# Queries, keys and probabilities of the mixers turned through HBM instead of on TensorE

## The chip, the core and the metric

One core of a Trainium2 chip runs the whole program. The metric is the device time of one execution in microseconds. The kernel before takes 2475.66 us (median of 3 runs, 2475.55 to 2479.15).

## The reference, cut to what matters

Two layers work on 256 tokens of width 2048. Each layer has a mixer, a cross-attention into 256 memory tokens and a feed-forward network (FFN), each added to `x`.

```python
# layer 0: proj = rms_norm(x) @ w_in_ab -> rq, rk, rv, rg (retention), nq, nk, nv (neighbourhood attention)
ret = rms_norm(fwd + bwd, ret_g) * silu(rg)              # 8 heads of 128, chunkwise retention both ways
na  = softmax(norm(nq) @ norm(nk).T * scale + bias) @ nv # 8 heads of 128
x = x + concat(ret, na) @ w_out_ab
# layer 1: proj = rms_norm(x) @ w_in_c -> q, k, v (8 heads, two queries and two keys of 128, values of 256)
a = softmax(q0 @ k0.T * scale + alibi) - lam * softmax(q1 @ k1.T * scale + alibi)
x = x + (rms_norm(a @ v, out_g) * (1 - lam_init)) @ w_out_c
# both layers: cross-attention (4 heads), then (silu(h @ w_g) * (h @ w_u)) @ w_ffn_out
```

A product on TensorE sums over the partitions, so the left operand must lie with its summed axis there. Projections come out with tokens on the partitions. Queries, keys, probabilities and head outputs therefore have to be turned before their next product.

## The kernel before, in words

**The products.** `gemm` (line 297) goes through 864 units. A unit is 256 rows of the weights by 512 columns, for both token tiles `t`: 12 matrix products of 128x128 by 128x512 (lines 321 to 323), since every operand is a high part and a low remainder (`hi`, `lo`; `wh`, `wl`) and three of the four partial products are summed. `prepare` (line 269) loads 1 MB of weights for two units (`raw`), casts a unit's high part on ScalarE (line 292, `wh`) and subtracts for the low part on VectorE (line 293, `wl`). It stands `LOOK` = 2 units ahead in the program. `wh` and `wl` have three buffers each, so the cast of unit k can start once TensorE is through with unit k-3, which is two units before unit k begins.

**The side work.** Everything between the products is a generator in `Side` (line 33). After each unit `pump` (line 63) lets one ready task make one step; a `yield n` puts the next step off by n units. At most `CAP` = 5 tasks are under way. `drain` finishes tasks at once where a later product needs them. The engines run their queues in order, so an instruction that waits holds all that stands behind it on its engine. The order in each queue is made when the program is built.

**The turn on TensorE.** `turn` (line 340) issues four 128x128 transposes into a PSUM tile `pt`. `heads_T` (line 459) does that twice for each group of queries or keys, `transpose_p` (line 541) once for a head's probabilities, `diff_head` (line 699) once more for a head's output in layer 1, `gate_T` (line 607) twice for a group of gated outputs. ScalarE and VectorE then make the high and low part out of `pt`.

**The move through HBM.** `regroup` (line 377) turns without TensorE, and before it serves the inputs of cross-attention and of the FFN's two projections (`feed`, `act_T`): VectorE transposes 32x32 squares (line 389, `zz`), SyncE writes them to HBM (line 391, `zd`), `LAND` = 2 units later GpSimd's queue reads them back by four DMAs, one for each 32 partitions (line 394), and `MOVE` = 5 units after the start ScalarE and VectorE make high and low part from `zz`.

**GpSimd's other duty.** `rsqrt_mean` (line 334) has the power -1/2 of each norm done on GpSimd, and VectorE's next instruction (line 487) waits for it.

Of the kernel before, what the change touches and what calls it, by code (L numbers as in the profile page):

```python
# [26 lines left out]
LAND, MOVE = 2, 5  # L27
# [5 lines left out]
class Side:  # L33
# [3 lines left out]
    CAP = 5  # L37
# [44 lines left out]
def trunk_kernel(  # L82
# [129 lines left out]
    def pair(which, name):  # L212
        hi = big.tile([P, 16, T], F32R, tag=f"{which}h", name=f"{name}h")
        lo = big.tile([P, 16, T], F32R, tag=f"{which}l", name=f"{name}l")
        return hi, lo
# [81 lines left out]
    def gemm(kts, src, epi, gate=None, steps=1, wide=False):  # L297
        hi, lo = src
        w2, rows, cols, order = plan[at["phase"]]
        at["phase"] += 1  # L300
        nu = 2 * len(rows)
        accs, left = {}, {}
        for b, u in order:
            side.drain((gate or {}).get(u, ()))
            if b not in accs:
                pools = ((ps_acc, f"acc{t}") for t in range(2))
                if wide and b in (2, 3):
                    pools = ((ps_t, "pt"), (ps_t, "pt")) if b == 2 else ((ps_a, "pa"), (ps_a, "pa"))
                accs[b] = [q.tile([P, NB], F32, tag=tag, name=f"acc{t}") for t, (q, tag) in enumerate(pools)]
                left[b] = nu  # L310
            while len(ahead) <= LOOK and at["unit"] < len(units):
                prepare()
            wh, wl = ahead.popleft()
            acc = accs[b]
            first, left[b] = left[b] == nu, left[b] - 1
            last = left[b] == 0
            for t in range(2):
                ts = slice(t * P, (t + 1) * P)
                for j in range(2):
                    kt = kts[u // 2] + 2 * (u % 2) + j  # L320
                    nc.tensor.matmul(acc[t], lhsT=hi[:, kt, ts], rhs=wh[:, j], start=first and j == 0, stop=False)  # L321
                    nc.tensor.matmul(acc[t], lhsT=hi[:, kt, ts], rhs=wl[:, j], start=False, stop=False)  # L322
                    nc.tensor.matmul(acc[t], lhsT=lo[:, kt, ts], rhs=wh[:, j], start=False, stop=last and j == 1)  # L323
            if last:
                epi(b, acc)
            side.pump(steps)
# [21 lines left out]
    def gained(dst, kt, src, g):  # L348
        hi, lo = dst[0][:, kt], dst[1][:, kt]
# [27 lines left out]
    def regroup(srcs, room=""):  # L377


        if room == "m8":  # L380
            both = m8.tile([P, 2, 4 * T], F32, tag="m8", name="zz")
            zt, zT = both[:, 0], both[:, 1]
        elif room:
            zt, zT = (qk.tile([P, 4 * T], F32, tag=room + x, name="zz") for x in "hl")
        else:
            zt, zT = (vp.tile([P, 4 * T], F32, tag="v" + x, name="zz") for x in "hl")
        zt = zt.rearrange("p (j k t b) -> p j k t b", j=4, k=4, t=2)
        for t in range(2):
            nc.vector.transpose(zt[:, :, :, t], srcs[t].rearrange("p (k j a) -> p j k a", j=4, a=32))
        zd = dram.tile([4, 32, 4, T], F32, name="zd")  # L390
        nc.sync.dma_start(zd.rearrange("i a j n -> (i a) (j n)"), zt.rearrange("p j k t b -> p (j k t b)"))
# [5 lines left out]
        return zT.rearrange("p (i k t b) -> p i k t b", i=4, k=4, t=2)  # L397
# [11 lines left out]
    def feed(dst, b, srcs, gi, layer, ssr, room):  # L409
# [5 lines left out]
        for k in range(4):  # L415
            g = gain(gi, layer, 4 * b + k)
            hi, lo = (x[:, 4 * b + k].rearrange("p (t i b) -> p t i b", t=2, i=4) for x in dst)
# [6 lines left out]
    def feed_x(dst, b, gi, layer, ssr, room=""):  # L424

        return [side.add(feed(dst, b, x_block(b), gi, layer, ssr, room))] * 2
# [32 lines left out]
    def heads_T(zs, dst, g):  # L459
# [21 lines left out]
    def normed_T(acc, rstd, gc, name, wait=4):  # L481
# [12 lines left out]
        return d, side.add(heads_T(zs, d, head_gain(gc)), wait)  # L494

    def plain_T(acc, rstd, name, mul):
        zs = evac(acc, rstd)
        d = turned(name)
        return d, side.add(heads_T(zs, d, mul), 3)
# [48 lines left out]
    def attend(g, h, dst, kt, bias=None):  # L548
# [10 lines left out]
        yield g.get("wait", 4)  # L559
        pT = transpose_p(pr)  # L560
# [5 lines left out]
        split(dst[0][:, kt], dst[1][:, kt], po)  # L566
# [40 lines left out]
    def gate_T(zs, oT, kt, g):  # L607
        for u in range(2):
            pt = turn(zs, u)
            gained_pair(part(oT, slice(kt + 2 * u, kt + 2 * u + 2)), pt, g)  # L610
            yield 0

    def retention_na(j, hT, rstd, oT, gate):
        groups = [{"n": 0} for gi in range(4)]
        groups[0]["tb"] = side.add(na_bias(j, 0, groups[0], hT[0][:, 4, 0:16].bitcast(F32)), 6)
        tails = []

        def epi(b, acc):
            if b < 12:
                gi, part = b // 3, b % 3  # L620
                g = groups[gi]
                if gi < 2:
                    if part == 0:
                        g["q"], g["tq"] = normed_T(acc, rstd, c_naq + j, "qT")
                    elif part == 1:
                        g["k"], g["tk"] = normed_T(acc, rstd, c_nak + j, "kT")
                        side.drain([g["tb"], small[0]])
                        heads = [side.add(attend(g, h, oT, 8 + gi * 4 + h, bias=g["bias"]), cond=prepared(g))
# [5 lines left out]
                elif part == 0:  # L634
                    side.drain(small)
                    g["q"], g["tq"] = plain_T(acc, rstd, "qT", 1.0)
                elif part == 1:
                    g["k"], g["tk"] = plain_T(acc, rstd, "kT", SCALE)
# [6 lines left out]
            else:  # L645
# [9 lines left out]
                tails.append(side.add(gate_T(zs, oT, gi * 4, head_gain(c_ret + j)), 2))  # L655
# [6 lines left out]
    def diff_head(g, hh, h, j, oT):  # L662
# [17 lines left out]
        yield 3  # L680
        aT = transpose_p(p0)
# [14 lines left out]
        for t in range(2):  # L696
            nc.vector.tensor_scalar(do[:, t], po[:, t], rr[:, t:t + 1], None, op0=ALU.mult)
# [8 lines left out]
    def diff_attention(j, hT, rstd, oT, gate):  # L706
        groups = [{} for _ in range(4)]

        def epi(i, acc):
            b, part = i // 3, i % 3  # L710
            g = groups[b]
            if part == 0:
                g["q"], g["tq"] = normed_T(acc, rstd, c_dq + j, "qT")
            elif part == 1:
                g["k"], g["tk"] = normed_T(acc, rstd, c_dk + j, "kT")
                g["tasks"] = [side.add(diff_head(g, hh, 2 * b + hh, j, oT), cond=prepared(g)) for hh in range(2)]
# [42 lines left out]
    for layer in range(2):  # L759
# [37 lines left out]
        tasks = [t for b in range(4) for t in feed_x(hT, b, 1, layer, ssr, ("", "", "qT", "m8")[b])]  # L797
# [15 lines left out]
        xo = (xo[:, 0], xo[:, 1])  # L813
# [6 lines left out]
        def epi_xo(b, acc):  # L820
# [3 lines left out]
            else:  # L824
                tasks.extend(feed_x(hT, b, 3, layer, ssr, ("", "", "qT", "kT")[b]))
# [4 lines left out]
        def act_T(aT, zs, kt):  # L830
            zT = yield from regroup(zs)
            for t in range(2):
                split(*(x[:, kt:kt + 4, t * P:(t + 1) * P].rearrange("p k (i b) -> p k i b", i=4) for x in aT),
                      zT[:, :, :, t].rearrange("p i k b -> p k i b"))
# [76 lines left out]
```

## Time and profile before

| what | value |
|---|---|
| time, median of 3 | 2475.66 us |
| profiled execution: time / span | 2475.84 us / 2474.1 us |
| TensorE busy | 2456.3 us (99%) |
| VectorE / ScalarE / GpSimd busy | 60% / 48% / 6% |
| DMA | 511.82 MB, mean 207 GB/s |
| granted TensorE clock | 1.000 |

The span runs from the first to the last instruction; 1.7 us lie around it. Busy is the time in which an engine has an instruction in work. TensorE's products overlap: one is recorded with some 390 ns although the next one starts 227 ns after it, so what a product costs is read from the distance of starts, not from its recorded length.

### The profile page before, as it was taken

How to read it: one execution, taken by the hardware profiler on the slowest of the kernel's cores; microseconds unless marked ns; L12 is line 12 of the kernel's file. 1: busy time of each engine (PE TensorE's matmuls, PEld its weight loads, DVE VectorE, ACT ScalarE, POOL GpSimd, SP SyncE). 2: the span in 40 equal slices, each digit the busy share in tenths (PEclk: the TensorE clock that was granted, in tenths of full speed). 3: DMA queues.
4: the chain of work that ended last, by engine and by line, in shares of the span. 5: the costliest groups of instructions: out<-in, count | busy, mean ns of one | idle time of the engine just before them, and what ended most of it. 6: DMA issues, size and time to landing. Idle time of an engine off the chain costs nothing.

```text
span 2474.1 us, 28641 instructions
## 1 busy us (share of the span) xinstructions
PE 2456.3 (99%) x11184; PEld 2037.1 (82%) x11184; DVE 1475.7 (60%) x1833; ACT 1187.0 (48%) x1538; POOL 138.2 (6%) x215
## 2 busy tenths in 40 slices
PE   8999999999999999999999999999999999999999
PEld 6888888888888888888888888888888888888887
DVE  6775565675655555555567766767655545555554
ACT  6554464564443444444455555655544444443443
POOL 1000001010000000000010000010100000000000
PEclk9999999999999999999999999999999999999999
DMA  8555567656765666566674555675766656665665
GB/s 288 177 169 179 175 226 245 214 192 213 233 216 200 205 212 225 194 198 226 225 241 164 170 170 168 212 249 171 237 222 210 215 188 214 228 206 200 207 217 175
DMA packets 250184, 511.82 MB, mean 207 GB/s; under 512 B 11328, under 2 KB 11968, under 8 KB 250048
## 3 DMA queue, kind: packets, MB, share of 16 engines
q1 hardware_dynamic: 239568, 484.47, 58.5%
q0 software_dynamic: 8320, 23.08, 4.1%
q10 hardware_dynamic: 2160, 2.44, 0.3%
q8 instruction: 87, 1.43, 0.2%
q14 instruction: 49, 0.40, 0.0%
HBM read 486.88 MB, written 23.07 MB: 206 GB/s over the span
## 4 chain that ended last, share of the span: by engine, by line
PE 92%; DMA 3%; DVE 3%; ACT 1%; POOL 1%; issue 0%; ACTq 0%; SPq 0%; POOLq 0%; DVEq 0%
PE acc L322 30%; PE acc L321 30%; PE acc L323 30%; DMA zz<-zd 2%; DVE wl L293 1%; DMA zd<-zz 1%; PE pt L345 1%; ACT wh L292 0%; PE pt L545 0%; PE pa_s L437 0%; PE pa_s L436 0%; DVE x_sb L741 0%; PE pa_s L435 0%; POOL zz L394 0%; PE pa_r L595 0%
## 5 line engine op out<-in xcount | busy, mean ns | idle before, releaser
L293 DVE TENSOR_TENSOR wl<-raw,wh 128x1024 fp32r<-128x1024 f32 (+1 forms) x865 | 1053.7, 1221 | 870.8 <-ACT wh L292 870.4
L292 ACT CAST wh<-raw 128x1024 fp32r<-128x1024 f32 (+1 forms) x865 | 909.1, 1051 | 1158.2 <-PE acc L323 1132.8
L322 PE MATMUL acc<-wl,hTfh 128*128 128x512 f32 x1408 | 547.9, 389 | 0.6 <-DVE wl L293 0.6
L323 PE MATMUL acc<-wh,hTfl 128*128 128x512 f32 x1408 | 547.7, 389 | 0.0
L321 PE MATMUL acc<-wh,hTfh 128*128 128x512 f32 x1408 | 547.7, 389 | 0.0
L321 PE MATMUL acc<-wh,hTh 128*128 128x512 f32 x832 | 332.0, 399 | 9.8 <-ACT wh L292 8.3
L322 PE MATMUL acc<-wl,hTh 128*128 128x512 f32 x832 | 325.7, 391 | 0.9 <-DVE wl L293 0.9
L323 PE MATMUL acc<-wh,hTl 128*128 128x512 f32 x832 | 325.8, 392 | 0.0
L322 PEld LDWEIGHTS acc<-wl,hTfh 128*128 128x128 f32 x1408 | 264.3, 188 | 56.2 <-DVE wl L293 1.4
L323 PEld LDWEIGHTS acc<-wh,hTfl 128*128 128x128 f32 x1408 | 264.3, 188 | 54.9
L321 PEld LDWEIGHTS acc<-wh,hTfh 128*128 128x128 f32 x1408 | 264.3, 188 | 54.9
L322 PE MATMUL acc<-wl,aTh 128*128 128x512 f32 x704 | 274.0, 389 | 0.2 <-DVE wl L293 0.2
L323 PE MATMUL acc<-wh,aTl 128*128 128x512 f32 x704 | 273.9, 389 | 0.0
L321 PE MATMUL acc<-wh,aTh 128*128 128x512 f32 x704 | 273.9, 389 | 0.0
L321 PEld LDWEIGHTS acc<-wh,hTh 128*128 128x128 f32 x832 | 157.2, 189 | 40.0 <-ACT wh L292 8.3
L323 PEld LDWEIGHTS acc<-wh,hTl 128*128 128x128 f32 x832 | 156.7, 188 | 34.0
L322 PEld LDWEIGHTS acc<-wl,hTh 128*128 128x128 f32 x832 | 157.2, 189 | 31.2 <-DVE wl L293 1.8
L394 POOL DMA_DIRECT2D zz<-zd x160 | 87.3, 552 | 1589.9 <-DMA zd<-zz 1410.9
L322 PEld LDWEIGHTS acc<-wl,aTh 128*128 128x128 f32 x704 | 132.1, 188 | 28.2 <-DVE wl L293 0.8
L321 PEld LDWEIGHTS acc<-wh,aTh 128*128 128x128 f32 x704 | 132.1, 188 | 27.5
L323 PEld LDWEIGHTS acc<-wh,aTl 128*128 128x128 f32 x704 | 132.1, 188 | 27.3
L321 PE MATMUL acc<-wh,oTh 128*128 128x512 f32 x256 | 100.2, 392 | 0.0
(189 smaller groups left out, 1940.3 us busy)
## 6 DMA issues: line engine op xcount, KB each, us to landing
raw<-in_w_ffn_in SPq DMA_DIRECT2D x176, 1024.0 KB, 5.1
raw<-in_w_ffn_out SPq DMA_DIRECT2D x88, 1024.0 KB, 5.1
raw<-in_w_in_ab SPq DMA_DIRECT2D x55, 1024.0 KB, 5.2
raw<-in_w_in_c SPq DMA_DIRECT2D x48, 1024.0 KB, 5.2
zd<-zz SPq DMA_DIRECT2D x40, 512.0 KB, 3.8
zz<-zd POOLq DMA_DIRECT2D x160, 128.0 KB, 5.4
raw<-in_w_out_ab SPq DMA_DIRECT2D x16, 1024.0 KB, 5.1
raw<-in_w_xkv SPq DMA_DIRECT2D x16, 1024.0 KB, 5.0
```

The costliest lines, as they stand in the source:

```text
L292: nc.scalar.copy(wh[:, js], raw[:, rs])
L293: nc.vector.tensor_sub(wl[:, js], raw[:, rs], wh[:, js])
L321: nc.tensor.matmul(acc[t], lhsT=hi[:, kt, ts], rhs=wh[:, j], start=first and j == 0, stop=False)
L322: nc.tensor.matmul(acc[t], lhsT=hi[:, kt, ts], rhs=wl[:, j], start=False, stop=False)
L323: nc.tensor.matmul(acc[t], lhsT=lo[:, kt, ts], rhs=wh[:, j], start=False, stop=last and j == 1)
L345: nc.tensor.transpose(pt[:, j, t * P:(t + 1) * P], srcs[t][:, c:c + P], ident)
L394: nc.gpsimd.dma_start(zT[32 * j:32 * j + 32].rearrange("a (i n) -> a i n", i=4), zd[:, :, j].rearrange("i a n -> a i n"))
```

## The change

`heads_T`, `attend`, `diff_head` and `gate_T` take a `room`. With a room they turn by `regroup` with `wait=SLOW` (8 units from start to the split; `gate_T`'s too); without one they turn on TensorE as before. Queries and keys of all four groups of layer 0 and of groups 0 to 2 of layer 1 go through HBM, as do the probabilities of the eight neighbourhood heads, the probabilities and outputs of heads 0 to 5 of layer 1, and the first group of gated outputs. Group 3 of layer 1 and the second gate group stay on TensorE. Squares of two 128-wide tiles (`nk=2`) are half as large as those before. `CAP` is 7. Operands (`pair`) become four tiles of four 128-row blocks; blocks of `oT` that aren't filled yet are the rooms. Two scalings in `diff_head` move from VectorE to ScalarE.

```diff
-LAND, MOVE = 2, 5
+LAND, MOVE, SLOW = 2, 5, 8
-    CAP = 5
+    CAP = 7
+    class Pair:
+        def blk(self, b):
+            if b not in self.blocks:
+                self.blocks[b] = tuple(big.tile([P, 4, T], F32R, tag=f"{self.which}{x}{b}", name=f"{self.name}{x}")
+                                       for x in "hl")
+            return self.blocks[b]
+    def regroup(srcs, room="v", nk=4, wait=MOVE):
+        zt, zT = room_for(room, nk * T)
+        zv = zt.rearrange("p (j k t b) -> p j k t b", j=4, k=nk, t=2)
+        for t in range(2):
+            nc.vector.transpose(zv[:, :, :, t], srcs[t].rearrange("p (k j a) -> p j k a", j=4, a=32))
+        zd = dram.tile([4, 32, 4, nk * 64], F32, tag=f"zd{nk}", name="zd")
+        nc.sync.dma_start(zd.rearrange("i a j n -> (i a) (j n)"), zt)
         yield LAND
         for j in range(4):
             nc.gpsimd.dma_start(zT[32 * j:32 * j + 32].rearrange("a (i n) -> a i n", i=4),
                                 zd[:, :, j].rearrange("i a n -> a i n"))
-        yield MOVE - LAND
+        yield wait - LAND
+    def split_moved(dst, zT):
+        for t in range(2):
+            split(*(x[:, :, t * P:(t + 1) * P].rearrange("p k (i b) -> p k i b", i=4) for x in dst),
+                  zT[:, :, :, t].rearrange("p i k b -> p k i b"))
-    def heads_T(zs, dst, g):
+    def heads_T(zs, dst, g, room=None):
+        if room:
+            zT = yield from regroup(zs, room, wait=SLOW)
+            if g is not None:
+                flat = zT.rearrange("p i k t b -> p (i k t b)")
+                nc.scalar.activation(flat, flat, AF.Copy, scale=g)
+            split_moved(dst, zT)
+            return
...
-        yield g.get("wait", 4)
-        pT = transpose_p(pr)
+        if room:
+            zT = yield from regroup([pr[:, t] for t in range(2)], room, 2, SLOW)
+            pT = tuple(pp.tile([P, 2, T], F32R, name="p" + x) for x in "hl")
+            split_moved(pT, zT)
+        else:
+            yield g.get("wait", 4)
+            pT = transpose_p(pr)
...
+        spare = [oT.which + x for x in "01"]
-                        g["q"], g["tq"] = normed_T(acc, rstd, c_naq + j, "qT")
+                        g["q"], g["tq"] = normed_T(acc, rstd, c_naq + j, "qT", spare[0])
...
+        def spare(b, x):
+            return oT.which + x if b < 3 else None
-                g["q"], g["tq"] = normed_T(acc, rstd, c_dq + j, "qT")
+                g["q"], g["tq"] = normed_T(acc, rstd, c_dq + j, "qT", spare(b, "3"))
...
-            nc.vector.tensor_scalar(p1[:, t], p1[:, t], r1[:, t:t + 1], None, op0=ALU.mult)
+            nc.scalar.activation(p1[:, t], p1[:, t], AF.Copy, scale=r1[:, t:t + 1])
...
+        if room:
+            zT = yield from regroup([do[:, t] for t in range(2)], room, 2, SLOW)
+            for e in range(2):
+                ze = zT[:, :, e].rearrange("p i t b -> p i (t b)")
+                nc.scalar.activation(ze, ze, AF.Copy, scale=head_gain(c_do + 2 * j + e))
+            split_moved(oT.at(2 * h, 2), zT)
+            return
```

On TensorE, where the queries of layer 0's first group are turned (z the normed queries, pt the PSUM tile), the kernel before has this between the end of a unit and the next unit:

```order
L322 MATMUL acc_554<-wl,hTh 128x512
L323 MATMUL acc_554<-wh,hTl 128x512
L345 MATMUL pt<-ident,z 128x128 x4
L321 MATMUL acc_553<-wh,hTh 128x512
L322 MATMUL acc_553<-wl,hTh 128x512
```

At the same place the changed kernel has:

```order
L335 MATMUL acc_564<-wl,hTh 128x512
L336 MATMUL acc_564<-wh,hTl 128x512
L334 MATMUL acc_563<-wh,hTh 128x512
L335 MATMUL acc_563<-wl,hTh 128x512
L336 MATMUL acc_563<-wh,hTl 128x512
```

The four transposes are gone from between the units; 50 such fours are gone from the whole queue (64 stand alone between two units before, 14 after), and the first scores of that group stand after 26 units instead of 21.

On ScalarE, in the same group, from the keys to the first head's probabilities (kTh the keys' high part, pr the probabilities, ph their high part, vh the values), before:

```order
L445 ACTIVATE kTh<-pt,gcol 128x512
L292 CAST wh<-raw 128x1024
L537 ACTIVATE pr,se<-pr,mx 128x256 x2
L292 CAST wh<-raw 128x1024
L537 ACTIVATE pr,se<-pr,mx 128x256 x2
L292 CAST wh<-raw 128x1024
L509 ACTIVATE vh<-acc_553,ssxr 128x512
```

In the changed kernel:

```order
L488 ACTIVATE zz<-zz,gcol 128x1024
L540 ACTIVATE vh<-acc_564,ssxr 128x512
L306 CAST wh<-raw 128x1024
L453 CAST kTh<-zz 128x4x128 x2
L306 CAST wh<-raw 128x1024 x2
L568 ACTIVATE pr,se<-pr,mx 128x256 x2
L306 CAST wh<-raw 128x1024
L568 ACTIVATE pr,se<-pr,mx 128x256 x2
L306 CAST wh<-raw 128x1024 x3
L453 CAST ph<-zz 128x2x128 x2
```

The reads of `zz`, which wait for a DMA, now stand among the casts of the weights. All 35 moves of the mixers stand so; from the VectorE transposes to ScalarE's first read there are 5 to 7 casts of the weights for a full square and 3 to 6 for a half one.

On GpSimd, at the start of layer 1 (rr the norm's power, rrd that of a head's output, zz<-zd the reads from HBM), before:

```order
L394 DMA zz<-zd 32x4x256 x4
L334 TENSOR_TENSOR rr<-rr,mhalf 128x8 x2
L334 TENSOR_TENSOR rrd<-rrd,mhalf 128x2 x2
L334 TENSOR_TENSOR rr<-rr,mhalf 128x8 x2
L334 TENSOR_TENSOR rrd<-rrd,mhalf 128x2 x2
```

In the changed kernel:

```order
L412 DMA zz<-zd 32x4x256 x4
L347 TENSOR_TENSOR rr<-rr,mhalf 128x8
L412 DMA zz<-zd 32x4x256
L347 TENSOR_TENSOR rr<-rr,mhalf 128x8
L412 DMA zz<-zd 32x4x256 x7
L412 DMA zz<-zd 32x4x128 x4
L347 TENSOR_TENSOR rr<-rr,mhalf 128x8
L412 DMA zz<-zd 32x4x128 x4
L347 TENSOR_TENSOR rrd<-rrd,mhalf 128x2
L412 DMA zz<-zd 32x4x256 x4
```

Reads that wait for `zd` now stand ahead of the powers in one queue, where before the powers had it to themselves.

## Rows read from the trace of the kernel before

**Rows 1.** The page: busy time of each engine, and the granted clock.

```profile
PE 2456.3 (99%) x11184; PEld 2037.1 (82%) x11184; DVE 1475.7 (60%) x1833; ACT 1187.0 (48%) x1538; POOL 138.2 (6%) x215
...
PEclk9999999999999999999999999999999999999999
```

**Rows 2.** Waits of TensorE: waited for, us in total, times, longest us.

```profile
PE acc L321 <- ACT wh L292: 8.3, 1, 8.3
PE acc L322 <- DVE wl L293: 2.2, 6, 0.5
PE pa_o L436 <- DVE pl L430: 1.6, 1, 1.6
PE acc L321 <- DVE z L475: 1.5, 2, 0.8
```

**Rows 3.** Groups by line and shape, TensorE, the transposes: xcount | busy us, mean ns | idle.

```profile
L345 PE MATMUL pt<-ident,z 128*128 128x128 f32 x160 | 23.6, 272 | 0.0
...
L545 PE MATMUL pt<-ident,pr 128*128 128x128 f32 x96 | 14.7, 272 | 0.0
...
L702 PE MATMUL pt<-ident,do 128*128 128x128 f32 x32 | 4.8, 272 | 0.0
...
L345 PE MATMUL pt<-ident,sg 128*128 128x128 f32 x16 | 2.4, 272 | 0.0
```

**Rows 4.** Timeline of TensorE in the FFN, first and thirteenth product: start us, us.

```profile
640.05 0.39 PE L321 MATMUL acc<-wh,hTfh 128*128 128x512 f32 x1
...
642.77 0.39 PE L321 MATMUL acc<-wh,hTfh 128*128 128x512 f32 x1
```

**Rows 5.** Timeline of TensorE in layer 0's mixer, a unit and its turn.

```profile
65.64 0.48 PE L321 MATMUL acc<-wh,hTh 128*128 128x512 f32 x1
65.96 0.39 PE L322 MATMUL acc<-wl,hTh 128*128 128x512 f32 x1
...
68.50 0.60 PE L345 MATMUL pt<-ident,z 128*128 128x128 f32 x4
68.85 0.48 PE L321 MATMUL acc<-wh,hTh 128*128 128x512 f32 x1
```

**Rows 6.** Timelines of VectorE, SyncE, GpSimd, ScalarE: one square of the FFN.

```profile
675.76 1.29 DVE L389 STREAM_TRANSPOSE zz<-sg 128x512 f32<-128x512 f32 x2
...
677.08 0.34 SPq L391 DMA_DIRECT2D zd<-zz  x1
...
681.36 2.17 POOL L394 DMA_DIRECT2D zz<-zd  x4 [40.04 <-DMA zd<-zz]
...
688.53 1.05 ACT L292 CAST wh<-raw 128x1024 fp32r<-128x1024 f32 x1 [1.67 <-PE acc L323]
689.48 1.14 ACT L429 CAST aTh<-zz 128x512 fp32r<-128x512 f32 x2
...
690.76 1.29 DVE L430 TENSOR_TENSOR aTl<-zz,aTh 128x512 fp32r<-128x512 f32 x2
```

**Rows 7.** The chain of waits where three squares follow each other: start us, us.

```profile
541.06 6.83 DMA zd<-zz
...
548.46 1.62 POOL zz L394 x3
550.08 9.15 DMA zz<-zd
...
559.34 0.52 ACT hTfh L419
559.88 2.20 DVE hTfl L421 x8
...
563.30 0.50 PE acc L322
```

**Rows 8.** Lines 394 and 391, all DMAs: length and time to landing, min/median/max.

```profile
L394 POOL DMA_DIRECT2D zz<-zd x160: 550/550/595, 402.9 to 2413.1; - x160
DMA to landing us min/median/max: 2.8/5.4/9.4
...
L391 SPq DMA_DIRECT2D zd<-zz x40: 338/338/339, 399.6 to 2406.9; - x40
DMA to landing us min/median/max: 2.6/3.8/7.3
```

**Rows 9.** Stretches (layer 0's mixer, then layer 1's): us, PE, PEld, DVE, ACT, POOL, clock, DMA, GB/s.

```profile
8.00:357.00 349.00, 346.00 (x1656) 288.23 (x1657) 225.26 (x323) 184.11 (x269) 18.75 (x17) 1.00 0.63 204
...
1263.00:1560.00 297.00, 295.71 (x1433) 246.91 (x1433) 205.72 (x313) 157.57 (x247) 21.07 (x19) 1.00 0.53 175
```

**Rows 10.** Timeline of VectorE and TensorE at the end of the first keys' norm.

```profile
62.29 1.29 DVE L475 TENSOR_TENSOR z<-acc,rr 128x512 f32<-128x512 f32 x2
...
56.03 0.47 PE L321 MATMUL acc<-wh,hTh 128*128 128x512 f32 x1 [0.72 <-DVE z L475]
```

**Rows 11.** Tile rr on GpSimd, and who waited for it (us, times).

```profile
L334 POOL TENSOR_TENSOR rr<-rr,mhalf x18: 1630/1636/2723, 53.3 to 1700.8; 128x8 f32<-128x8 f32 x18
...
  DVE rr L487: 27.8, 16
```

More of the change, by code (lines that the diff above doesn't have):

```diff
@@ L209, in lambdas, with __init__, at @@
         yield
[L212 to L215, printed above, removed]
+    class Pair:
+        def __init__(self, which, name):
+            self.which, self.name, self.blocks = which, name, {}
+        def blk(self, b):
[3 more added lines that the diff above has]
+            return self.blocks[b]
+        def at(self, kt, n=None):
+            k = kt % 4
+            return tuple(x[:, k if n is None else slice(k, k + n)] for x in self.blk(kt // 4))
+    pair = Pair
     side = Side()
@@ L319, in gemm @@
                 for j in range(2):
[L320 to L323, printed above, removed]
+                    hi, lo = src.at(kts[u // 2] + 2 * (u % 2) + j)
+                    nc.tensor.matmul(acc[t], lhsT=hi[:, ts], rhs=wh[:, j], start=first and j == 0, stop=False)
+                    nc.tensor.matmul(acc[t], lhsT=hi[:, ts], rhs=wl[:, j], start=False, stop=False)
+                    nc.tensor.matmul(acc[t], lhsT=lo[:, ts], rhs=wh[:, j], start=False, stop=last and j == 1)
             if last:
@@ L493, in normed_T, with plain_T @@
         d = turned(name)
-        return d, side.add(heads_T(zs, d, head_gain(gc)), wait)
-    def plain_T(acc, rstd, name, mul):
+        return d, side.add(heads_T(zs, d, head_gain(gc), room), 0 if room else 4)
+    def plain_T(acc, rstd, name, mul, room):
         zs = evac(acc, rstd)
         d = turned(name)
-        return d, side.add(heads_T(zs, d, mul), 3)
+        return d, side.add(heads_T(zs, d, mul, room))
     def prepared(g):
@@ L605, in ret_head, with gate_T @@
                 head_scale(ro[t], ro[t], rr, t)
[L607 to L611, printed above, removed]
+    def gate_T(zs, oT, kt, g, room):
+        yield from heads_T(zs, oT.at(kt, 4), g, room)
     def retention_na(j, hT, rstd, oT, gate):
+        spare = [oT.which + x for x in "01"]
         groups = [{"n": 0} for gi in range(4)]
-        groups[0]["tb"] = side.add(na_bias(j, 0, groups[0], hT[0][:, 4, 0:16].bitcast(F32)), 6)
+        groups[0]["tb"] = side.add(na_bias(j, 0, groups[0], hT.blk(1)[0][:, 0, 0:16].bitcast(F32)), 6)
         tails = []
@@ L654, in epi @@
                     zs.append(sg)
-                tails.append(side.add(gate_T(zs, oT, gi * 4, head_gain(c_ret + j)), 2))
+                tails.append(side.add(gate_T(zs, oT, gi * 4, head_gain(c_ret + j), ("qT", None)[gi]), 2 * gi))
         gemm(KT4, hT, epi, gate=gate)
@@ L712, in epi @@
             if part == 0:
-                g["q"], g["tq"] = normed_T(acc, rstd, c_dq + j, "qT")
+                g["q"], g["tq"] = normed_T(acc, rstd, c_dq + j, "qT", spare(b, "3"))
             elif part == 1:
-                g["k"], g["tk"] = normed_T(acc, rstd, c_dk + j, "kT")
-                g["tasks"] = [side.add(diff_head(g, hh, 2 * b + hh, j, oT), cond=prepared(g)) for hh in range(2)]
+                g["k"], g["tk"] = normed_T(acc, rstd, c_dk + j, "kT", spare(b, "2" if b < 2 else "3"))
+                g["tasks"] = [side.add(diff_head(g, hh, 2 * b + hh, j, oT, oT.which + str(b + 1) if b < 3 else None), cond=prepared(g)) for hh in range(2)]
             else:
@@ L796, in trunk_kernel @@
         ssr = new_ss("ssx")
-        tasks = [t for b in range(4) for t in feed_x(hT, b, 1, layer, ssr, ("", "", "qT", "m8")[b])]
+        tasks = [t for b in range(4) for t in feed_x(hT, b, 1, layer, ssr, ("v", "v", "qT", "m8")[b])]
         g = {"wait": 3}
```

63 lines of the change are left out of this document (32 added, 31 removed).

## The prediction

> **What bounds the kernel now.** I read the page first: TensorE is busy for 2456.3 of 2474.1 us at a granted clock of 1.0 (the 2.4 GHz level) in every slice, VectorE 60%, ScalarE 48% [rows 1]. So the next view is who makes TensorE wait: four rows, of which the first (8.3 us) is the start of the program; the others add up to 5.3 us [rows 2]. The kernel is bounded by what stands in TensorE's queue. A busy TensorE can hide what an instruction costs, since products overlap, so the timeline comes third, and there the reader should look at distances of starts. In the FFN the thirteenth product starts 642.77 - 640.05 = 2.72 us after the first [rows 4]: a unit without side work. In layer 0's mixer a unit that ends in a turn takes 68.85 - 65.64 = 3.21 us [rows 5]. A turn of four transposes therefore costs 3.21 - 2.72 = 0.49 us of TensorE. The four take 0.35 us until the next product starts (68.85 - 68.50), and the rest goes to that product, whose successor comes 0.32 us after it instead of 0.23 [rows 5]. The group rows would mislead: 272 ns for one transpose [rows 3] is its recorded length, not its cost.
>
> **What is removed.** By the order 50 fours leave the stretches between units: 28 of queries and keys (14 groups of two), 14 of probabilities, 6 of head outputs, 2 of gated outputs; 200 of the 304 transposes in [rows 3]. On the path that sets the end that is 50 x 0.49 = 24.5 us. Nothing else in TensorE's queue changes in number, and the products that stay keep their shapes. The profiled execution took 2475.84 us, 0.2 us over the median of the three runs, so without any new wait the time would be 2475.84 - 24.5 = 2451.3 us.
>
> A page speaks of the same operation: the Trainium skill's "TensorE: Matmul & The Clock Gate", section "Part 4: PE-mode transpose", gives some 275 ns for a 128x128 transpose inside a kernel. The recorded length agrees [rows 3], but the distance of starts does not [rows 5]; by the page 200 x 0.275 = 55 us would go, an estimate that gives 2421 us.
>
> **What is added on the other engines.** 35 moves: 15 full squares (as large as those of before) and 20 half ones. VectorE gets 1.29 us of transposes and 1.29 us of subtractions for a full square [rows 6] and about half for a half one; even with nothing set off for what it no longer reads from PSUM that is 15 x 2.58 + 20 x 1.29 = 65 us. In the two mixers VectorE is busy for 225.3 + 205.7 = 431 of 646 us and ScalarE for 342 [rows 9]; 65 more makes 77%, and ScalarE's share (casts of 1.14 us for a full square, scalings, the two moved from VectorE) stays under 65%. That work is hidden by the products. The bytes are hidden too: 15 x 1 MB + 20 x 0.5 MB on a DMA share of 0.63 and 0.53 [rows 9]. What can cost is waiting, in three queues.
>
> **The first keys of each layer.** Their scores are the one place where TensorE takes up a square almost as soon as it lands. In layer 0 the keys' norm ends at 62.29 + 1.29 = 63.6 us, and unit 16 starts at 56.03 [rows 10]. The transposes of queries and keys put 2 x 1.29 us in front: 66.2. A quiet square needs 689.48 - 677.05 = 12.4 us from the end of its transposes to ScalarE's read [rows 6]; one among close neighbours needed 559.34 - 541.06 = 18.3 [rows 7]. Then come scaling (1.05, as the cast of the same shape), casts (1.14) and the last subtraction (0.65): ready between 81.4 and 87.3. TensorE reaches the scores 10 units after unit 16, at 83.2. It waits for 0 to 4.1 us; with two squares 6 us apart I take the middle, 1.8. Layer 1 opens in the same pattern (units 456 to 466): together 3.6 us.
>
> **The half squares.** Behind ScalarE's read of a square stand the casts of the weights, and behind those the products. ScalarE's cast is two units ahead, so a read may stand for 5.44 - 1.05 = 4.4 us before TensorE notices. In the FFN the read stands six casts behind the transposes and comes 12.4 us after them, 3.9 us under six units. By that measure a read three casts behind comes after 4.3 us, four casts behind after 7.0, five after 9.7. In the order 5 half squares stand at three, 10 at four, 5 at five or six. No row shows a half square: its bounds are the shortest landings with GpSimd's four issues, 2.6 + 0.6 + 2.17 + 2.8 = 8.2 us [rows 6, 8], and the 18.3 of [rows 7]. I take 10.5, since the nearest row is the quiet full square (12.4), with the same number of issues and half the bytes. At four casts 10.5 - 7.0 = 3.5 lies inside the reserve. At three 10.5 - 4.3 - 4.4 = 1.8 is left; but the mixers' units are longer (297 / 96 = 3.1 us [rows 9]), which gives back up to 1.1 over three. I take 1.0 each: 5 us. The full squares of later groups stand at 5 to 7 and have units to spare before their scores: nothing.
>
> **GpSimd's queue.** Reads that wait for `zd` now stand ahead of the norms' powers. VectorE already waits 27.8 / 16 = 1.7 us for each power [rows 11] and its lead is 5.44 - 1.05 - 1.23 = 3.2 us, so a short hold is hidden; I take nothing, with 0 and the rival below as ends. SyncE's `zd` stands between the loads of `raw`, six casts ahead of use as the FFN's do now, where TensorE shows no wait for a load [rows 2].
>
> Sum: 2475.84 - 24.5 + 3.6 + 5 = 2459.9, say **2460 us**, its own range 2452 to 2468.
>
> **The rivals.**
> (a) *Late half squares on ScalarE; slower.* If a half square takes 14 us (between the quiet row and [rows 7]), those at three casts lose 14 - 8.7 = 5.3 each and those at four 14 - 11.4 = 2.6 each: 26 + 26, with 5 for the first keys 57, which gives 2508 us. It decides from about 12 us on: 5 x 3.3 + 10 x 0.6 + 3.6 = 26 eats the gain. For it: [rows 7], and that in layer 1 two heads and the next group's queries and keys move within some 25 us. Against: there three full squares lay 5 us apart, and the mixers have the lightest DMA share [rows 9]. 10 in 100.
> (b) *Powers held behind reads.* Eight norms have their power directly behind reads in GpSimd's queue. Each hold is up to the median landing of `zd`, 3.8 [rows 8]: 3.8 + 1.7 - 3.2 = 2.3 us for TensorE, 18 in all, hence 2478 us, no change. For it: the queue is in order. Against: the reads are issued two units after `zd`, which is longer than 3.8. 11 in 100.
> (c) *The moves are as short as their best.* With 8.2 us for any square no read outlasts the reserve and the first keys are in time: 2451 us. Against: medians of 3.8 and 5.4 [rows 8]. 15 in 100. The Trainium skill has this in "DMA: Bandwidth & Descriptors", section "Anatomy of one DMA — SWDGE (gpsimd) path": 2.0 us plus bytes at 436 GB/s, by which 64 KB would land in 2.15 us and the sum would again be 2451, an estimate. The trace does not agree: 128 KB took 5.4 us in the median and 2.8 at the least.
> (d) *The transposes cost their recorded length.* 200 x 0.272 = 54 us less, 2421. Against it is every distance of starts in [rows 5]. 2 in 100.
> (e) *Later side work piles up.* The scores come some 5 units later than before, and what is unfinished at the end of a projection is drained without products in between. The order shows no such heap; the last head of layer 1 is turned at unit 547 instead of 543, its reader is at 549. Were a whole drain exposed there, with one full square's 12.4 us, it would be 2472 us. 2 in 100.
>
> **How the numbers follow.** The forecast has 60 in 100. What a measurement of this kernel can tell from no change is about 0.2%, 5 us: below 2470.7 is faster, above 2480.6 slower. Faster: 60 + 15 + 2 + a rest of 1 from (b) = 78. Same: 10 of (b) and (e) = 12. Slower: (a), 10. The range from 2450 to 2476 leaves out (a), (d) and most of (b) and is wide because the half square has no row.
>
> **What would show it.** TensorE's groups: 104 transposes are left, and a plain unit is still 2.72 us. Waits of TensorE: first scores of each layer 0 to 4 us, casts of the weights (wh, wl) together about 5. The reads and writes of half squares land in the time between them that I took (10.5 us from transposes to landing); over 12 the forecast falls to (a). Powers on GpSimd: VectorE's wait for rr stays near 1.7 each; at 4 or more (b) holds. If the units around the moves grow above 2.72 us without a named wait, the forecast is wrong in a way that none of these has.

## The result and the profile after

The changed kernel takes 2487.31 us (median of 4 runs, 2482.08 to 2490.55), the kernel before on the same chip 2475.61. The ratio is 1.0041, 95% interval 1.0029 to 1.0052: slower, where 2460 us and faster was forecast. The profiled execution took 2482.08 us, 6.2 more than that of before. One execution of e1 below (5048.88 us) and one of e2 (4118.33 us, at a mean clock of 0.556) lie far off and are left out of the ratios; e2's only trace is of that one, so nothing is read from it.

TensorE's own work shrank as planned. First the page's row of busy times and its clock (PE is TensorE, PEld its weight loads, DVE VectorE, ACT ScalarE, POOL GpSimd), then the groups of transposes that are left (columns as in [rows 3]):

```profile
PE 2443.0 (98%) x10984; PEld 2018.3 (81%) x10984; DVE 1493.0 (60%) x1885; ACT 1211.9 (49%) x1609; POOL 223.0 (9%) x355
...
PEclk9999999999999999999999999999999999999999
```

```profile
L358 PE MATMUL pt<-ident,z 128*128 128x128 f32 x48 | 7.1, 273 | 0.1
L576 PE MATMUL pt<-ident,pr 128*128 128x128 f32 x40 | 6.3, 272 | 0.0
...
L358 PE MATMUL pt<-ident,sg 128*128 128x128 f32 x8 | 1.4, 279 | 0.2 <-DVE sg L687 0.2
L748 PE MATMUL pt<-ident,do 128*128 128x128 f32 x8 | 1.2, 272 | 0.0
```

Of the 304 transposes of [rows 3] 104 are left, 200 are gone, and PE has 200 instructions fewer than in [rows 1]. The time came back, most of it as waits: TensorE's span less its busy time is 2480.3 - 2443.0 = 37.3 us, and was 2474.1 - 2456.3 = 17.8. Here are TensorE's waits, then ScalarE's (waited for: us in total, times, longest us):

```profile
PE acc L334 <- ACT wh L306: 17.7, 7, 8.4
PE acc L335 <- DVE wl L307: 11.0, 21, 0.8
PE pa_s L460 <- DVE kTl L454: 1.7, 2, 1.0
```

```profile
ACT zz L741 <- DMA zz<-zd: 28.4, 6, 6.7
...
ACT zz L488 <- DMA zz<-zd: 21.5, 9, 7.7
...
ACT ph L453 <- DMA zz<-zd: 17.0, 7, 5.1
ACT do L736 <- POOL rrd L347: 10.6, 8, 3.0
```

In [rows 2] TensorE waited once for `wh` (8.3 us, the start of the program) and 2.2 us for `wl`. Now it waits 9.4 us more for `wh` and 8.8 more for `wl`. And ScalarE, which casts `wh`, stands 66.9 us at squares that have not landed: 28.4 at head outputs (line 741), 21.5 at queries and keys (488), 17.0 at probabilities (453). The fourth line (736) came with the scalings that moved to ScalarE; it is no part of the loss, for e1 below keeps it (9.4 us) and loses nothing.

The worst place shows how the one becomes the other. It is the keys of layer 0's second group. First the chain of waits (start us, us), then the timelines of ScalarE and TensorE (start us, us, engine, line, operation, in brackets the idle time before and what ended it), then TensorE's part in stretches of 5 us (us, PE, PEld, DVE, ACT, POOL, granted clock, DMA share, GB/s):

```profile
141.07 6.77 DMA zd<-zz
...
148.41 1.35 POOL zz L412 x3
150.09 10.02 DMA zz<-zd
```

```profile
151.46 1.05 ACT L306 CAST wh<-raw 128x1024 fp32r<-128x1024 f32 x1 [1.67 <-PE acc L336]
160.22 1.15 ACT L488 ACTIVATE zz<-zz,gcol 128x1024 f32<-128x1024 f32 x1 [7.71 <-DMA zz<-zd]
161.28 1.25 ACT L540 ACTIVATE vh<-acc,ssxr 128x512 fp32r<-128x512 f32 x2
162.42 1.04 ACT L306 CAST wh<-raw 128x1024 fp32r<-128x1024 f32 x1
```

```profile
163.51 0.80 PE L334 MATMUL acc<-wh,hTh 128*128 128x512 f32 x1 [3.93 <-ACT wh L306]
...
165.79 0.63 PE L334 MATMUL acc<-wh,hTh 128*128 128x512 f32 x1
166.22 0.63 PE L335 MATMUL acc<-wl,hTh 128*128 128x512 f32 x1
```

```profile
155.00:160.00 5.00, 4.58 (x21) 3.46 (x19) 0.00 (x0) 0.00 (x0) 0.00 (x0) 1.00 0.97 253
160.00:165.00 5.00, 1.03 (x2) 0.52 (x3) 2.92 (x4) 4.78 (x7) 0.00 (x0) 0.84 0.06 22
165.00:170.00 5.00, 5.00 (x12) 3.90 (x13) 3.19 (x4) 1.52 (x3) 0.00 (x0) 0.50 0.33 86
```

The square landed 19.1 us after its transposes (141.04 to 160.1), beside weight loads at a DMA share near 1. ScalarE reached its read 6 casts behind the transposes by its queue (two of them ran before VectorE was through) and stood 7.71 us. On release the scaling and two casts of the values came first; the cast of the weights that would have been due at 151.46 + 2.72 = 154.2 started at 162.42, 8.2 us late. TensorE noticed 3.93 of them. Then a second price fell due: the granted clock went to 0.84 and 0.50 (the 1.2 GHz level), and products followed each other at 0.43 us (165.79 to 166.22) instead of 0.23 (2.72 / 12 by [rows 4]). By their starts two units and the one after them took 7.8 us more than such units take otherwise (6.81 and 6.12 instead of 2.72, and 3.74, where the next one with the same six products of scores takes 3.46). 4.4 of that was waiting (3.93 and 0.46), the other 3.4 the clock. Nowhere else in this execution was the granted clock under 1.00.

VectorE's wait for the norms' powers did not grow (28.0 us in 16 times here, 27.8 in [rows 11]).

### The profile page after: what moved, and what is told of

Same layout as the page of the kernel before. It is cut to its first block, busy times and chain, and to the rows that moved or that the text cites. A ratio compares the mean times of both kernels' runs of the same rounds, so it can differ in the third digit from the quotient of the medians.

```text
span 2480.3 us, 28762 instructions
## 1 busy us (share of the span) xinstructions
PE 2443.0 (98%) x10984; PEld 2018.3 (81%) x10984; DVE 1493.0 (60%) x1885; ACT 1211.9 (49%) x1609; POOL 223.0 (9%) x355
## 4 chain that ended last, share of the span: by engine, by line
PE 78%; DMA 9%; DVE 6%; issue 3%; POOL 2%; ACT 2%; ACTq 0%; POOLq 0%; DVEq 0%
PE acc L335 26%; PE acc L336 25%; PE acc L334 25%; DMA zz<-zd 5%; DMA zd<-zz 3%; DVE wl L307 2%; POOL zz L412 1%; ACT wh L306 1%; POOL rr L347 1%; DVE zz L407 1%; DMA x_sb<-in_x 1%; DVE z L506 0%; DVE ss L502 0%; PE pa_s L460 0%; DMA dec<-in_ret_decay_bwd 0%
## 5 line engine op out<-in xcount | busy, mean ns | idle before, releaser
L412 POOL DMA_DIRECT2D zz<-zd x300 | 165.2, 557 | 1880.1 <-DMA zd<-zz 1598.2
L334 PEld LDWEIGHTS acc<-wh,aTh 128*128 128x128 f32 x704 | 132.2, 188 | 27.8 <-ACT wh L306 0.4
L335 PE MATMUL acc<-wl,oTh 128*128 128x512 f32 x256 | 99.8, 390 | 0.8 <-DVE wl L307 0.8
```

The source lines that it names most:

```text
L334: nc.tensor.matmul(acc[t], lhsT=hi[:, ts], rhs=wh[:, j], start=first and j == 0, stop=False)
L335: nc.tensor.matmul(acc[t], lhsT=hi[:, ts], rhs=wl[:, j], start=False, stop=False)
```

## The experiments

Theory A: the loss is ScalarE standing at squares that have not landed, with the casts of the weights behind it. Rival B: the transfers themselves (DMA traffic, SyncE's and GpSimd's queues). Rival C: the other edits (blocks, cap, scalings). Each ratio is against the kernel before on the same chip, with its 95% interval.

**e1. All turns back on TensorE, the rest of the change kept.**

```diff
     def heads_T(zs, dst, g, room=None):
+        room, g = None, 1.0 if g is None else g
...
     def attend(g, h, dst, kt, bias=None, room=None):
...
+        room = None
...
     def diff_head(g, hh, h, j, oT, room):
+        room = None
```

The first group of gated outputs gets no room either, and the waits in front of the turns are those of before (4, 3 and 2 units).

> All of the mixers' turns are back on TensorE, with the waits that they had before; the new blocks of the weight loads, the cap of seven and the scalings of queries and keys on ScalarE stay. Theory A (what was lost is ScalarE's standing at squares that have not landed, with the casts of weights behind it): nothing is left that stands, so 2475 us, within 4 us of the kernel before. Rival B (the added traffic and SyncE's queue): the traffic is gone too, so also 2475 us. Rival C (the blocks, the cap or the scalings, whatever the squares do): it stays above 2480 us.

Measured: 2474.34 us, ratio 1.000 (0.9991 to 1.0009). Rival C falls: without the moves, blocks, cap and scalings cost nothing that shows (the interval reaches 2 us to either side).

**e2. Read what VectorE transposed, not what lands.**

```diff
         yield wait - LAND
+        zT = zt if wait == SLOW else zT
```

> Every square of the change is issued with all its DMAs, but the high and low parts are made from what VectorE has transposed in place, not from what lands from HBM, so that no reader waits for a DMA (the output is not the reference's: the 32x32 blocks stay where they were). Theory A: the 24.35 us of turns are kept and the standing is gone: about 2452 us, and ScalarE's rows with a wait for zz from the DMA are gone for these squares. Rival B (traffic and SyncE's queue): the DMAs are all still there, so it stays at 2480 us or above. Rival C: 2480 us or above too.

Measured: 2465.01 us, 0.9956 (0.9943 to 0.9970). By the two ratios it lies some 21 us below the changed kernel, and none of that is traffic, since all DMAs are there. But it is not 2452: some 14 us have another cause.

**e3. The moves beside the turns, read by nobody.**

```diff
-    CAP = 7
+    CAP = 14
...
+    def idle(srcs, room, nk):
+        yield from regroup(srcs, room, nk, SLOW)
...
+            side.add(idle(zs, room, 4))
...
+            side.add(idle([pr[:, t] for t in range(2)], room, 2))
...
+            side.add(idle([p0[:, t] for t in range(2)], "m8", 2))
...
+            side.add(idle([do[:, t] for t in range(2)], room, 2))
```

> The turns are on TensorE as before the change, and beside them the same squares are written to and read from HBM with nobody who reads what lands (the queue of side work may hold 14 entries here, so that the added ones find room). Theory A: nobody stands, so 2475 to 2479 us; the added transposes on VectorE may cost a few tenths each. Rival B: the traffic alone makes weight loads late: 2490 us or above, since the 24.35 us of turns are back as well. Rival C: as e1, above 2480 us.

Measured: 2527.10 us, 1.0206 (1.0192 to 1.0220), in the span of Rival B (2490 us or above), but at least in part for another reason. The added tasks take steps of the side work, heads are left to the end of layer 1's projection and drained there in a heap: two units there last 19.0 and 12.8 us by their starts. The run does not separate traffic from heap, and e5 takes its place.

**e4. Twelve units of slack instead of eight.**

```diff
-LAND, MOVE, SLOW = 2, 5, 8
+LAND, MOVE, SLOW = 2, 5, 12
```

> Only the declared wait from the writing of a square to its scaling goes from eight units to twelve. By the program's counting alone a square would have four units, 11 us, more to land: then the standing goes and the time is 2452 to 2465 us. But in the order of the instructions ScalarE's read of a square stands no more casts behind the transposes than before in most places (four for a half square, six for a full one, as with eight). If that order is what counts, as Theory A has it, the time stays within 6 us of the changed kernel's 2487 us. Rival B: no change either. e2 and e3 tell A from B; this run tells whether the declared number reaches the chip.

Measured: 2497.65 us, 1.0089 (1.0075 to 1.0102), 10 us worse than the changed kernel; I had expected it within 6. ScalarE still stands 55.1 us at the three lines above (66.9 in the changed kernel), at reads that come as early as before: between a square's transposes and its first read 3 casts of the weights start in the median for a half square and 4 for a full one, in both kernels. What the declared number does reach is the program's own deadlines: the heads that it puts off meet the drain at unit 40. ScalarE there, and the stretch (columns as above):

```profile
144.42 0.71 ACT L453 CAST ph<-zz 128x256 fp32r<-128x256 f32 x2 [6.42 <-DMA zz<-zd]
```

```profile
140.00:145.00 5.00, 0.58 (x2) 0.30 (x2) 3.44 (x11) 0.58 (x2) 2.50 (x3) 0.71 0.59 169
145.00:150.00 5.00, 4.82 (x16) 4.14 (x17) 1.60 (x5) 1.45 (x3) 1.50 (x3) 0.61 0.36 107
```

**e5. As e2, and no transfer at all for the squares of the change.**

```diff
+        if wait == SLOW:
+            yield wait
+            return zt.rearrange("p (i k t b) -> p i k t b", i=4, k=nk, t=2)
         zd = dram.tile([4, 32, 4, nk * 64], F32, tag=f"zd{nk}", name="zd")
```

> As e2, the high and low parts are made from what VectorE has transposed in place, but now the squares of the change are neither written to HBM nor read back (their 50 turns stay off TensorE; the output is not the reference's). VectorE and ScalarE do the same work as in e2. e2 kept 10 us of the 24.35 us of turns; this run divides the 14 us that it lost. If the transfers took them (traffic beside the weight loads, SyncE's and GpSimd's queues): 2450 to 2453 us. If ScalarE's and VectorE's own work for the squares took them: 2463 to 2467 us, as e2.

Measured: 2465.98 us, 0.9964 (0.9952 to 0.9977), the same as e2. So the transfers cost nothing that shows, and Rival B falls as far as these two runs can tell. What is left shows in e5's trace first of all as TensorE's waits for VectorE (columns as above). Two places: VectorE's wait at one, the stretch at the other.

```profile
PE acc L335 <- DVE wl L307: 10.8, 7, 4.4
```

```profile
DVE lprod L202 <- DMA lrow<-in_lambda_k: 6.6, 1, 6.6
```

```profile
1460.00:1465.00 5.00, 2.27 (x6) 1.79 (x7) 5.00 (x8) 3.24 (x4) 0.00 (x0) 0.79 0.21 45
```

At the first VectorE stands 6.6 us at the small loads of layer 1's lambda, TensorE 4.4 us behind it; the kernel before stands 2.9 us at the same load, the changed one not at all, so up to some 4 us of e5's time is this accident. At the second VectorE is busy for all of 5 us with a norm, transposes and subtractions, and `wl` comes 3.0 us late.

**e6. ScalarE's reads pinned.** Each read of a landed square is queued behind the newest cast that the program has issued.

```diff
-            nc.scalar.copy(wh[:, js], raw[:, rs])
+            at["cast"] = nc.scalar.copy(wh[:, js], raw[:, rs]).ins
...
-            split_moved(pT, zT)
+            with tc.issue_after(at["cast"]):
+                split_moved(pT, zT)
```

That is the place of the neighbourhood heads; the other three (scaling and split of queries, keys and gated outputs, of layer 1's probabilities, of its head outputs) get the same.

> The changed kernel with one thing more: each of ScalarE's reads of a landed square stands in ScalarE's order behind the newest cast of weights that the program has issued by then. Behind the transposes of a half square now stand 6 to 8 casts (4 to 6 before, mostly 4), behind those of a full square 7 to 17 (5 to 7 before). Theory A (ScalarE stands at squares that have not landed, and the casts behind it are late): the 22 us between the changed kernel and e2 come back, so 2462 to 2468 us, under both kernels. Rival B (the traffic alone): 2480 us or above. Rival D (the read now comes too late for the matmuls that use it, which keep their place): TensorE waits at the scores and products instead, and it stays at 2475 us or above.

Measured: 2465.49 us, 0.9959 (0.9946 to 0.9971). This is the changed kernel with every square, every byte and the declared eight units, and by the two ratios some 20 us came back. What moved is the reads in ScalarE's queue and, behind them, their subtractions in VectorE's; TensorE's queue is the same but for some 40 of its 10984 instructions. ScalarE's waits at the same three places, then TensorE's at the casts:

```profile
ACT ph L453 <- DMA zz<-zd: 3.9, 1, 3.9
...
ACT zz L745 <- DMA zz<-zd: 3.7, 1, 3.7
...
ACT zz L489 <- DMA zz<-zd: 3.1, 2, 1.7
```

```profile
PE acc L334 <- ACT wh L306: 10.6, 4, 8.1
PE acc L335 <- DVE wl L307: 5.5, 8, 0.8
```

ScalarE stands 10.7 us instead of 66.9. The squares themselves landed no sooner: half ones 11.3 us after their transposes in the median, nine of 20 over 12 (10.0 and six in the changed kernel). But 5 casts now start before a half square's read in the median instead of 3, and 6 instead of 4 before a full one's. So Theory A is shown for these 20 us; for the rest of the loss it is not. The keys of the worst place now (ScalarE's timeline):

```profile
158.06 1.05 ACT L306 CAST wh<-raw 128x1024 fp32r<-128x1024 f32 x1 [1.66 <-PE acc L336]
159.01 1.15 ACT L489 ACTIVATE zz<-zz,gcol 128x1024 f32<-128x1024 f32 x1
160.19 1.14 ACT L453 CAST kTh<-zz 128x512 fp32r<-128x512 f32 x2
161.24 1.05 ACT L306 CAST wh<-raw 128x1024 fp32r<-128x1024 f32 x1
```

No wait stands before the scaling, and the casts keep their pace. One place was left: the second head's probabilities in layer 1 waited for `m8`, which both heads used, so its read stood four casts behind late transposes. ScalarE waited 3.9 us, TensorE 3.2, the granted clock was 0.66 in the next 5 us, and the unit took 9.2 us. The expectation of e9 puts the loss at 6.5, against a plain unit; a unit with the same twelve products of a head takes 4.2 to 4.3 undisturbed, so it was about 5.

**e7 and e8. One kind of square alone.**

e7, in `attend` and in `diff_head`:

```diff
+        room = None
```

e8, in `heads_T`, with the waits and the gated outputs as in e1:

```diff
+        room, g = None, 1.0 if g is None else g
```

> Only queries, keys and the first gate group go through HBM (18 of the 50 turns counted in full squares' pairs, with 7.8 to 9 us less TensorE time for them); probabilities and head outputs are turned on TensorE as before the change. Theory A, by where the changed kernel's ScalarE stands: 21.5 us of standing at the scaling of queries and keys and the one clock fall of 8.5 us in all stay, 17 and 28.4 us at half squares go. So the gain in turns is eaten here: 2470 to 2478 us. If the half squares are what costs, 2466 us. If the full squares are the whole of it: 2485 us.

> Only probabilities and head outputs go through HBM; queries, keys and the gate group are turned on TensorE as before the change. Theory A: the standing at probabilities (17.0 us on ScalarE) and at head outputs (28.4 us) stays, and part of it reaches TensorE: 2472 to 2482 us. If the loss of the change is all in the full squares: 2459 us. If it is all in the half squares: 2487 us or above.

Measured: e7 2480.96 us, 1.0024 (1.0015 to 1.0034); e8 2492.68 us, 1.0074 (1.0060 to 1.0088). The count in e7's expectation was wrong: 15 full squares are 30 turns, 14.7 us, not 18 turns. So e7 lost 2481.0 - 2475.8 + 14.7 = 19.9 us and e8, with 20 turns (9.8 us), 2492.7 - 2475.8 + 9.8 = 26.7. Both kinds lose more than they gain, and no kind alone is the culprit. Both runs lie above the spans that I gave for Theory A, and e8 lies where I had put "all in the half squares". The two losses add to 46.6, the whole change lost 36, so each run has costs of its own: VectorE stands 5.9 us at the lambda load in e7, and in e8 TensorE waits 4.8 us for queries and keys that are to be turned (2.3 at the longest), which it does not in e1.

**e9 to e12. Towards a version that beats both.** e9 is e6 with two buffers in turn:

```diff
-    zT = yield from regroup([p0[:, t] ...], "m8", 2, SLOW)
+    zT = yield from regroup([p0[:, t] ...], ("m8", room)[hh], 2, SLOW)
-    zT = yield from regroup([do[:, t] ...], room, 2, SLOW)
+    zT = yield from regroup([do[:, t] ...], ("m8", room)[hh], 2, SLOW)
```

> e6, and in the second mixer the two heads of a group use two buffers in turn (the shared m8 for one head's probabilities and outputs, the spare block of operands for the other's), where both heads' probabilities went through m8 one after the other. In e6 the second head's probabilities had only four casts behind their transposes (they waited for m8), and at one place ScalarE stood 3.9 us and TensorE lost 6.5 us with a fall of its clock; now six or seven casts stand there. Theory A: that place goes, 2458 to 2463 us. If it was an accident of one execution, 2464 to 2467 us as e6.

Measured: 2462.87 us, 0.9946 (0.9933 to 0.9960). The place is gone. The gain over e6, 2.6 us by the medians, is not clear of the scatter of the runs (2461 to 2468 and 2459 to 2466).

e10 is e9 with `SLOW` = 9; e11 is e9 with `yield 1` after the split in `heads_T`.

> As e9 with nine units of slack declared instead of eight, which now reach ScalarE's order: one cast more behind nearly every square (7 to 9 behind half squares). Theory A: whatever still stood for want of time goes, so within 3 us of e9 or under it. If later reads make the matmuls that use them late (rival D), or the side work piles up at the end of a mixer as it did with twelve, above e9 by 4 us or more.

> As e9, and one step of side work lies between the read of queries or keys and the scores that use them. In e6 TensorE lost 2.7 us at the first keys of the first mixer and 0.9 us at those of the second, waiting for parts that ScalarE had just begun; the scores now come 1.4 units later there. If that wait is what those units cost: 2 to 3.5 us under e9. If the side work that is moved back by it costs as much: the same as e9 within 1.5 us.

Measured: e10 2480.60 us, 1.0014 (1.0005 to 1.0023); e11 2473.08 us, 0.9988 (0.9979 to 0.9997). Both miss to the slow side: later is no better than earlier. In e11 the wait at the first keys is gone, but the last two heads of the first group meet the drain at unit 40, and units 38 to 40 take 18.2 us. In e10, at TensorE's longest wait behind the start, a read on GpSimd waits for its buffer, the power of a norm stands behind it, and VectorE and TensorE behind that (waits at 1450 to 1464 us, then the stretch):

```profile
POOL zz L412 <- ACT ph L453: 8.0, 1, 8.0
...
DVE rr L519 <- POOL rr L347: 5.0, 1, 5.0
...
PE pa_d L461 <- DVE pl L454: 4.2, 1, 4.2
```

```profile
1460.00:1465.00 5.00, 4.02 (x16) 3.63 (x17) 3.70 (x6) 0.95 (x4) 0.43 (x1) 0.66 0.90 309
```

This place explains some 6 of the 18 us by which e10 lies over e9 (9.4 and 3.5 us for two units, where 4.2 and 2.7 are usual); the others are not taken apart.

e12 takes the other way out for the first keys: it turns them, and them alone, on TensorE again.

```diff
-                        g["k"], g["tk"] = normed_T(acc, rstd, c_nak + j, "kT", spare[1])
+                        g["k"], g["tk"] = normed_T(acc, rstd, c_nak + j, "kT", spare[1] if gi else None, 8)
```

The 8 is the wait in units before the turn.

> As e9, but the first keys of layer 0, whose scores follow at once, are turned on TensorE again (two turns, 0.98 us), with eight units of wait; all other squares stay moved. In e9 the first scores of layer 0 cost 5.1 us in the profiled execution: 2.6 us of waiting for keys and a granted clock of 0.84 and 0.81 in the ten microseconds around it. If that wait is the price of a square that is used as soon as it lands, it goes: 2 to 4 us under e9, 2458 to 2461 us. If the queries, moved one block earlier, are then the late ones, the same as e9 within 1.5 us.

Measured: 2458.59 us (2456.46 to 2461.56), 0.9933 (0.9919 to 0.9947), under both kernels and in the span that was expected. The interval overlaps that of e9, so the 4.3 us between their medians are likely, not certain. At the first scores, e9 and then e12 (stretches):

```profile
85.00:90.00 5.00, 2.44 (x8) 1.71 (x7) 2.87 (x4) 4.08 (x5) 0.00 (x0) 0.84 0.12 29
90.00:95.00 5.00, 5.00 (x25) 4.35 (x24) 3.28 (x5) 1.93 (x5) 0.00 (x0) 0.81 0.55 193
```

```profile
85.00:90.00 5.00, 5.00 (x29) 4.35 (x28) 3.02 (x4) 2.66 (x6) 0.00 (x0) 1.00 0.64 213
90.00:95.00 5.00, 5.00 (x24) 4.13 (x23) 4.92 (x13) 2.66 (x7) 0.37 (x1) 1.00 0.30 86
```

TensorE's waits in the whole of e12 are down to the start of the program and 8 us:

```profile
PE acc L334 <- ACT wh L306: 8.8, 2, 8.3
PE acc L335 <- DVE wl L307: 4.5, 7, 0.8
```

## Why the prediction was wrong

**The 24.5 us of turns: right as far as the runs tell.** 200 transposes are gone, and a plain unit still takes 2.72 us by its starts. e12, with few waits left and 48 of the 50 fours gone, lies 16.4 us under the kernel before; 48 x 0.49 would be 23.5, and the 7 us between are open.

**The step that failed: "At four casts 10.5 - 7.0 = 3.5 lies inside the reserve", and with it "The full squares of later groups ...: nothing".** I priced 5 us for five half squares and, but for the two first keys (3.6), nothing for the other squares. ScalarE stood 66.9 us; TensorE's waits at `wh` and `wl`, which were to be about 5 us, grew by 18.2. In the profiled execution 6.2 + 24.5 = 30.7 us came back instead of 8.6, in the median of all runs about 36. Of the 30.7, 19.5 are TensorE's added idle time (37.3 - 17.8) and 11.2 are added busy time (2443.0, where 2456.3 - 24.5 = 2431.8 was due), some 3.4 of which went to the clock at the worst place; the other 7.8 are not taken apart. The parts of the failed step:

- *The landing was sized right in the middle only.* From the end of the transposes to the last landing the 20 half squares took 10.0 us in the median (10.5 assumed), but 7.7 to 16.0; six of them lie over 12. The 15 full ones took 12.9 in the median, 12.0 to 19.1. A price of the form "time minus reserve, but not below zero" cannot be put on a median: the late ones pay and the early ones give nothing back. Rival (a) had the mechanism, at 14 us for every half square, and so 2508 us.
- *The reserve was right, but the square's own work was left out of it.* At the worst place the cast was 8.2 us late and TensorE waited 3.93, so the reserve was 4.3, as in the prediction (4.4). But the 8.2 are 7.7 of standing and 2.2 of work that ScalarE does first on release, less the 1.7 that it would have idled before the cast.
- *What the wait does to the clock was no term at all.* After a wait of some 4 us the granted clock fell to 0.50 in the next 5 us, and the units after it paid again. In the profiled execution that was the smaller part, 3.4 us; the slower executions paid more, for one thousandth of the mean clock is 2.5 us of 2480 (an estimate). Executions of the changed kernel at mean clocks of 0.999, 0.997, 0.996 and 0.997 took 2482.1, 2485.0, 2489.6 and 2490.6 us.
- *That the scores came later was no excuse.* I cleared the full squares by the distance to their scores. What the wait holds up is not the scores but the casts in the same queue, and these are due every unit.

**The eight units.** I counted the reads from the order (three to six casts behind half squares). What I did not ask was why eight declared units gave four casts. e4 and e6 answer it: the number sets when the program issues the read, the order on ScalarE is made apart from it, and in these runs only the tie to a cast carried the slack over. Then, with 6 to 8 casts behind half squares by the order, little standing is left (10.7 us in e6).

**First keys: near.** 1.8 us a layer were forecast; in layer 0 the wait for them was 1.6 us (0.5 and 1.05), and the unit took 2.1 us more than the next one with the same products; in layer 1 it was 0.7. The 1.8 was not the middle that the prediction calls it: the middle of 81.4 and 87.3 lies 1.15 us behind 83.2, that of 0 and 4.1 is 2.05. In other orders it was more: 2.6 us and a fall of the clock in e9, and e12, which removes it, is 4.3 us faster by the medians.

**Rival (b), powers held:** not in the changed kernel; VectorE's wait for them stayed at 28.0 us. It did appear in e10 (5.0 us at once), though there the read waited for its buffer and not for `zd`. **Rival (c):** the shortest squares (7.7 us) are under the 8.2 I took, but the median decides nothing here. **Rival (d):** no run came near 2421 us; e12, the fastest, took 2458.59. **Rival (e):** no unit of the changed kernel took longer than the 6.8 us of the worst place, so no drain stood exposed; drains did in e3, e4 and e11. **Reads of 64 KB:** the Trainium skill's "DMA: Bandwidth & Descriptors", section "Anatomy of one DMA — SWDGE (gpsimd) path", gives a fit by which the 64 KB of one of a half square's four reads would land in 2.15 us, an estimate. The 80 such reads of the changed kernel took 2.2 at the least, which agrees, and 4.6 in the median, which does not.

**Open:** why e2, e5 and e6 keep some 14 us of the loss is shown at places of e5 and e6 only (the lambda load, a busy VectorE, late probabilities), not summed; e12 still keeps 7. And whether the traffic costs a few us could hide behind the lambda load in e5.

## What to carry to other kernels

Where an engine with periodic work (casts, evacuations) also reads what a DMA lands, count how many periods stand between issue and read in that engine's own queue, and compare it with the slowest landing in the trace, not the median. A slack that is declared in program order may not reach the engine's queue: here it took a tie to an instruction in that queue. More of it is not better, since deadlines and buffers further on are then met instead (e4, e10). A square that is used as soon as it lands was, by the medians of e9 and e12, cheaper turned on TensorE.

## What the runs showed of the hardware

- A wait of TensorE of 2.6 to 4.4 us cost 1.4 to 1.8 times its length where the granted clock then fell to 0.50 (the 1.2 GHz level), by the starts of the units against undisturbed ones: 7.8 us for 4.4 in the changed kernel (163.5 to 170 us), 4.4 for 2.6 in e9, 5.0 for 3.2 in e6, 6.0 for 4.2 in e10. Two waits near 1406 us of the changed kernel (2.28 and 0.76, with one product between) left the clock at 1.00 and cost 3.6 us. The stretches of the changed kernel, e9, e10 and again the changed kernel:

```profile
163.50:170.00 6.50, 6.03 (x13) 4.42 (x14) 4.68 (x5) 3.02 (x5) 0.00 (x0) 0.50 0.26 66
```

```profile
88.50:91.50 3.00, 3.00 (x11) 2.54 (x10) 2.19 (x3) 0.59 (x1) 0.00 (x0) 0.50 0.68 203
```

```profile
1461.40:1464.60 3.20, 3.20 (x13) 2.91 (x13) 2.30 (x3) 0.95 (x4) 0.03 (x1) 0.50 0.95 302
```

```profile
1405.00:1410.00 5.00, 2.66 (x10) 1.99 (x11) 3.99 (x6) 5.00 (x8) 0.00 (x0) 1.00 0.23 80
```

- Small loads can land as late as large ones: the loads of lambda's four rows took 3.0 to 12.4 us in e5 beside weight loads, the 128 KB reads of [rows 8] 2.8 to 9.4.
